# Attention as one tied stream of matmuls in a hybrid layer kernel (scores, transposes and value products in a fixed rotation, output weights per unit)

## The chip, the cores and the metric

One core of a Trainium2 chip runs the whole kernel. The metric is device time in microseconds (us); lower is better. The kernel before was timed three times, and its median is the figure of reference.

## What is computed

One layer over 1024 latent tokens of width 1024 and 256 context tokens: conditioned norm, one input projection, then two groups of heads side by side, one output projection, and a mixture of 16 experts. The part that the change touches is the attention of the latent tokens and what runs beside it:

```python
def attend_blocked(q, k, v):          # 8 query heads, 2 key heads, head width 64, 1280 keys
    ...
    def one_block(qblk):
        s = jnp.einsum('bkgqd,bksd->bkgqs', qblk, k).astype(jnp.float32) * scale
        p = jax.nn.softmax(s, axis=-1).astype(v.dtype)
        return jnp.einsum('bkgqs,bksd->bkgqd', p, v)
...
    # head group B: gated DeltaNet, chunked scan, once per direction
    v_new = u_c - jnp.einsum('bhck,bhkv->bhcv', w_c, s)
    s_next = s * gl_c[..., None, None] + jnp.einsum('bhck,bhcv->bhkv', kd_c, v_new)
    o = jnp.einsum('bhck,bhkv->bhcv', qd_c, s) + jnp.einsum('bhij,bhjv->bhiv', qk_c, v_new)
...
    y = rmsnorm(o, o_norm_w) * jax.nn.silu(z)
    y_lat = jnp.concatenate([att_lat, dn_lat], axis=-1) @ w_out
```

## The kernel before

The kernel is written against a tile framework. Each engine has one queue that it works off strictly in order. The framework fills the queues in the order of the program, except that an instruction whose buffer is not yet free at that point stands back while later instructions of other streams go ahead, so the streams of one engine are mixed. `tc.issue_after` adds an order between two instructions of one engine without a semaphore.

The stages are: modulation and input projection (up to some 405 us), attention beside the DeltaNet scan (to about 705), attention beside the preparation of the output weights (to about 755), attention beside the first four output tiles (to about 870), the other output tiles and the choice of tokens, then the experts.

**Attention** is 16 calls of `att_group(j, hp)`: four blocks of 256 queries times four pairs of heads. A group is four *units* (`i`, `a`), 128 queries of one head each. In a unit TensorE (PE) makes the scores in three pieces (L1153, two matmuls each, into one of four buffers of the PSUM bank "a"), VectorE (DVE) takes each piece to SBUF with its running minimum (L1156, then L1158), ScalarE (ACT) takes the exponential of the whole row (L1159), PE transposes it in pieces of 4, 4 and 2 blocks (L1163, into one of two buffers of bank "t"), and ACT copies each piece out (L1164). At the group's end 20 value products (L1170) add into a buffer of bank "t"; they come in pairs that fill the two halves of the array (`tile_position`). The trace shows each as two instructions. The four `prob` buffers let scores run up to four units in front.

**Queries.** `att_q(j + 1)` is called in the group with `hp == 1` and `j < 3`. `query_split` makes its rotated and split queries by a chain on DVE (L481 to L503, with twelve small instructions of the inverse root between), then PE transposes them in four batches into bank "t" (L1123), the bank that attention's transposes and value products use.

**DeltaNet.** Ten steps `st`, each with two directions (`dn_step`), put on PE per direction the merges (lines 910 to 945, up to 64x64), then L977, L983, L992, L1005 and L1011. Between these stand results of DVE (L979, L988, L996) and ACT. One attention group is written behind each step. `tick` draws pieces of a side stream (`dn_wave`, DVE, lines 868 to 877) in between. From `st == 7` on `dn_out` norms two finished tiles: a sum, squares, an inverse root and a product on DVE (L1032 to L1048), four transposes per tile on PE (L1051), a copy on ACT (L1052) and a store.

**Output weights.** `out_weights` yields 16 pieces. Each loads a 128x512 slice, multiplies it by the gate row on DVE (L1214), takes its upper part on ACT (L1215) and the rest on DVE (L1216). The gate row of each half is loaded and added first (L1210). All 16 pieces are drawn by one `tick(16)` between attention groups 10 and 11 (counted from 0), behind `dn_out(7, 0)`. Groups 12 to 15 run beside `out_next`, which puts the output matmuls of one tile (lines 1298 to 1300) on PE.

Of the kernel before, what the change touches and what calls it, by code (L numbers as in the profile page):

```python
# [10 lines left out]
F32 = mybir.dt.float32  # L11
# [22 lines left out]
P = 128  # L34
# [8 lines left out]
DH = 4  # L43
# [41 lines left out]
class Layer:  # L85
# [51 lines left out]
    def build(self):  # L137
# [20 lines left out]
        for st in range(NT):  # L158
# [862 lines left out]
    def dn_out(self, *tiles):  # L1021
# [61 lines left out]
    def att_open(self):  # L1083
# [5 lines left out]
        self.att = {}  # L1089
# [40 lines left out]
    def att_group(self, j, hp):  # L1130
        nc = self.nc
        v = nc.vector
        tp = self.tp
        if hp == 1 and j < 3:
            self.att_q(j + 1)
        QT, rs = self.att[j]
        if hp == 0:
            self.OT = self.tw.tile([P, 4, 256], F32, name="OT", bufs=1)
        OT = self.OT
        kv = hp // 2  # L1140
        PT = [(self.tw if n == 2 else tp).tile([P, 512 * n], F32, name=f"PT{n}", tag=f"PT{n}", bufs=2)
              .rearrange("p (x a i q) -> p x a i q", x=n, a=2, i=2) for _, n in self.KG]
        for i in range(2):
            for a in range(2):
                h = 2 * hp + a
                pr = self.tw.tile([P, TOK], F32, name="prob", bufs=4)
                mn = self.tw.tile([P, 4], F32, name="mn", bufs=6)
                for y, (tag, c0, w) in enumerate((("a", 0, 448), ("a", 448, 416), ("a", 864, 416))):
                    ps = self.bank(tag)
                    for k0 in range(0, w, 512):  # L1150
                        ks = slice(c0 + k0, c0 + min(k0 + 512, w))
                        for x in range(2):
                            nc.tensor.matmul(ps[:, k0:min(k0 + 512, w)], QT[:, h, i], self.KTs[:, kv * 2 + x, ks],  # L1153
                                             start=x == 0, stop=x == 1)

                    v.tensor_scalar(pr[:, c0:c0 + w], ps[:, :w], -1.0, 3e38, op0=ALU.mult, op1=ALU.min,  # L1156
                                    accum_out=mn[:, y:y + 1])
                v.tensor_reduce(mn[:, 3:4], mn[:, 0:3], axis=AX.X, op=ALU.min)  # L1158
                nc.scalar.activation(pr, pr, AF.Exp, bias=mn[:, 3:4], scale=-1.0, accum_out=rs[:, a, hp, i:i + 1])  # L1159
                for g, (k0, n) in enumerate(self.KG):  # L1160
                    pt = self.bank("t")
                    for x in range(n):
                        nc.tensor.transpose(pt[:, x * P:(x + 1) * P], pr[:, (k0 + x) * P:(k0 + x + 1) * P], self.ident)  # L1163
                    nc.scalar.activation(PT[g][:, :, a, i], pt[:, :n * P].rearrange("p (x q) -> p x q", x=n), AF.Copy)  # L1164
# [643 lines left out]
```

## Time and profile before

| | us |
|---|---|
| three runs | 1531.51, 1533.72, 1539.18 |
| median | 1533.72 |
| the profiled execution | 1532.3 |
| its span, first to last instruction | 1530.6 |

The profiled execution is 1.4 us below the median, and 1.7 us of its time lie around the span. In a profile's row "busy" is time in which the engine works on an instruction, from decode to the last write, so neighbours overlap; the distance between the starts of two rows is what an instruction costs its queue. PE is the matmul engine, PEld its weight load, PEclk the granted share of TensorE's clock of 2.4 GHz.

### The profile page before, as it was taken

What the parts mean: (1) busy time and instruction counts of PE and PEld (TensorE: products, weight loads), DVE (VectorE), ACT (ScalarE), POOL (GpSimd) and SP (SyncE); (2) the same over time, 40 slices, a digit from 0 to 9 for tenths busy, and PEclk for the clock granted to TensorE, in tenths of its full rate; (3) what the DMA queues carried; (4) which work ended last, traced back from release to release, by engine and by line L of the source; (5) the groups of instructions that cost most, each with busy time, mean ns of one, the idle gap of its engine ahead of it and who ended that gap; (6) DMA issues with size and microseconds to landing.
All of it is one profiled execution on the core that took longest, in us unless ns stands there. A gap on an engine that the chain in (4) does not pass through costs nothing.

```text
span 1530.6 us, 25513 instructions
## 1 busy us (share of the span) xinstructions
PE 1446.1 (94%) x9444; PEld 1180.8 (77%) x9444; DVE 1170.2 (76%) x2424; ACT 962.9 (63%) x1602; POOL 167.4 (11%) x184
## 2 busy tenths in 40 slices
PE   4999999998799999999699997999999999999996
PEld 1887687898787878887577774788888888888885
DVE  1834668798685888568743588999999999999995
ACT  1824545654474446667754533788888888888883
POOL 0000000101311121110000101111111111111101
PEclk7899999999999899999899998999999999999998
DMA  9356836788735466554421565989999999999991
GB/s 343 120 182 215 264 119 190 213 280 272 218 102 175 136 182 186 157 172 152 138 70 56 182 245 222 378 296 393 393 398 392 395 395 395 393 387 376 385 377 29
DMA packets 170792, 381.59 MB, mean 249 GB/s; under 512 B 46063, under 2 KB 106235, under 8 KB 143147
## 3 DMA queue, kind: packets, MB, share of 16 engines
q1 hardware_dynamic: 158496, 338.88, 61.9%
q0 software_dynamic: 9792, 37.36, 7.9%
q10 hardware_dynamic: 2379, 3.72, 0.7%
q8 instruction: 74, 1.21, 0.3%
q14 instruction: 51, 0.42, 0.1%
HBM read 324.07 MB, written 55.84 MB: 248 GB/s over the span
## 4 chain that ended last, share of the span: by engine, by line
PE 75%; DVE 9%; DMA 6%; issue 4%; ACT 4%; SPq 1%; POOL 0%; POOLq 0%; ACTq 0%; DVEq 0%
PE ps_m L1631 33%; PE ps_a L1153 4%; PE ps_t L1163 4%; PE ps_t L1170 4%; PE ps_s L444 3%; PE ps_s L446 3%; PE ps_s L445 3%; PE ps_t L1631 2%; PE ps_d L1300 2%; PE ps_d L1298 2%; PE ps_d L1299 2%; PE ps_s L436 1%; PE ps_s L437 1%; PE ps_s L438 1%; PE ps_d L977 1%
## 5 line engine op out<-in xcount | busy, mean ns | idle before, releaser
L1631 PE MATMUL ps_m<-ehi,xx 128*128 128x512 f32 x1024 | 258.0, 394 | 1.0 <-DVE xx L1568 1.0
L1631 DVE TENSOR_TENSOR elo<-eraw,ehi 128x2048 fp32r<-128x2048 f32 x102 | 231.2, 2288 | 18.5 <-ACT ehi L1631 18.0
L1631 ACT ACTIVATE ehi<-eraw 128x2048 fp32r<-128x2048 f32 x105 | 201.3, 1919 | 56.1 <-PE ps_m L1631 43.5
L1631 PEld LDWEIGHTS ps_m<-ehi,xx 128*128 128x128 f32 x1024 | 188.7, 188 | 38.4 <-ACT xf L1564 1.1
L1631 PE MATMUL ps_m<-elo,xx 128*128 128x512 f32 x512 | 137.4, 390 | 0.0
L1631 PE MATMUL ps_m<-ehi,hx 128*128 128x512 f32 x512 | 129.7, 395 | 0.0
L1156 DVE TENSOR_SCALAR_CACHE_REDUCE prob<-ps_a 128x416 f32<-128x416 f32 (+1 forms) x192 | 110.1, 596 | 18.9 <-PE ps_a L1153 14.4
L1631 DVE TENSOR_TENSOR elo<-fraw,ehi 128x2048 fp32r<-128x2048 f32 x51 | 115.8, 2288 | 9.1 <-ACT ehi L1631 9.1
L1164 ACT ACTIVATE PT<-ps_t 128x512 f32<-128x512 f32 (+1 forms) x192 | 93.9, 526 | 38.9 <-PE ps_t L1163 36.8
L1153 PE MATMUL ps_a<-kts,QT 128*128 128x416 f32 (+1 forms) x384 | 111.3, 398 | 5.2 <-DVE prob L1156 5.1
L1631 ACT ACTIVATE ehi<-fraw 128x2048 fp32r<-128x2048 f32 x51 | 97.8, 1918 | 24.1 <-PE ps_m L1631 21.0
L1631 PEld LDWEIGHTS ps_m<-elo,xx 128*128 128x128 f32 x512 | 96.1, 188 | 20.4
L1631 PEld LDWEIGHTS ps_m<-ehi,hx 128*128 128x128 f32 x512 | 94.0, 188 | 18.2
L436 PE MATMUL ps_s<-whi,hh 128*128 128x256 f32 (+1 forms) x336 | 100.0, 299 | 4.1 <-DVE zz L629 4.1
L1163 PE MATMUL ps_t<-consts,prob 128*128 128x128 f32 x640 | 101.1, 285 | 1.0 <-ACT PT L1164 0.6
L438 PE MATMUL ps_s<-whi,hl 128*128 128x256 f32 (+1 forms) x336 | 97.6, 295 | 0.2 <-DVE hl L413 0.2
L437 PE MATMUL ps_s<-wlo,hh 128*128 128x256 f32 (+1 forms) x336 | 97.3, 292 | 0.0
L444 PE MATMUL ps_s<-hh,whi 128*128 128x512 f32 (+1 forms) x256 | 94.6, 370 | 0.0
L1159 ACT ACTIVATE prob<-prob,mn 128x1280 f32<-128x1280 f32 x64 | 87.3, 1365 | 10.4 <-DVE mn L1158 10.1
L446 PE MATMUL ps_s<-hh,wlo 128*128 128x512 f32 (+1 forms) x256 | 93.5, 365 | 0.0
L445 PE MATMUL ps_s<-hl,whi 128*128 128x512 f32 (+1 forms) x256 | 93.5, 365 | 0.0
L1776 POOL DMA_INDIRECT out_x<-ey,idx x16 | 52.0, 3252 | 342.4 <-DVE ey L1631 342.4
(432 smaller groups left out, 3099.0 us busy)
## 6 DMA issues: line engine op xcount, KB each, us to landing
eraw<-in_w_up SPq DMA_DIRECT2D x38, 1024.0 KB, 10.1
eraw<-in_w_down SPq DMA_DIRECT2D x32, 1024.0 KB, 7.4
eraw<-in_w_gate SPq DMA_DIRECT2D x31, 1024.0 KB, 8.7
wmod<-in_w_mod SPq DMA_DIRECT2D x24, 1024.0 KB, 6.1
fraw<-in_w_down SPq DMA_DIRECT2D x21, 1024.0 KB, 8.0
fqraw<-in_w_gate SPq DMA_DIRECT2D x16, 1024.0 KB, 8.9
fraw<-in_w_gate SPq DMA_DIRECT2D x16, 1024.0 KB, 7.0
fraw<-in_w_up SPq DMA_DIRECT2D x14, 1024.0 KB, 10.6
```

The costliest lines, as they stand in the source:

```text
L436: self.nc.tensor.matmul(ps[:, :n], self.hh[:, k, ts], hi[:, k, a:a + n], start=st, stop=False)
L437: self.nc.tensor.matmul(ps[:, :n], self.hh[:, k, ts], lo[:, k, a:a + n], start=False, stop=False)
L438: self.nc.tensor.matmul(ps[:, :n], self.hl[:, k, ts], hi[:, k, a:a + n], start=False, stop=en)
L444: self.nc.tensor.matmul(ps[:, :n], hi[:, k, a:a + P], self.hh[:, k, ts], start=st, stop=False)
L445: self.nc.tensor.matmul(ps[:, :n], hi[:, k, a:a + P], self.hl[:, k, ts], start=False, stop=False)
L446: self.nc.tensor.matmul(ps[:, :n], lo[:, k, a:a + P], self.hh[:, k, ts], start=False, stop=en)
L1153: nc.tensor.matmul(ps[:, k0:min(k0 + 512, w)], QT[:, h, i], self.KTs[:, kv * 2 + x, ks], start=x == 0, stop=x == 1)
L1156: v.tensor_scalar(pr[:, c0:c0 + w], ps[:, :w], -1.0, 3e38, op0=ALU.mult, op1=ALU.min, accum_out=mn[:, y:y + 1])
L1159: nc.scalar.activation(pr, pr, AF.Exp, bias=mn[:, 3:4], scale=-1.0, accum_out=rs[:, a, hp, i:i + 1])
L1163: nc.tensor.transpose(pt[:, x * P:(x + 1) * P], pr[:, (k0 + x) * P:(k0 + x + 1) * P], self.ident)
L1164: nc.scalar.activation(PT[g][:, :, a, i], pt[:, :n * P].rearrange("p (x q) -> p x q", x=n), AF.Copy)
L1631: i = fn(*args, **kw)
```

## The change

The attention is cut into `att_unit`, `att_scores`, `att_rows` (transposes and copies), `att_values` and `att_end`. All its matmuls on PE go through `queue("pa", ...)`, which ties each behind the one before it in the order of the program. The order is a rotation: piece `y` of the scores of a unit, then piece `y` of the transposes of the unit two in front of it. The value products of a group come in the third unit of the next group, behind its first piece of scores. Where values were written as a loop of their own at the group's end, they now run beside the next step of DeltaNet. `dn_out` is cut into `dn_norm` (all that DVE does, the eight products L1050 too) and `dn_rows` (transposes, copy, store). For tiles (7, 0), `dn_rows` is placed behind the last value product that group 11 issues. The output weights are drawn per unit: 1.5 pieces ahead of each unit of group 10 (6 pieces), 2.5 ahead of each of group 11 (10 pieces).

```diff
         self.prep, self.credit = self.out_weights(), 0
-        self.att_group(*ga.pop(0))
-        self.dn_out(7, 0)
-        self.tick(16)
+        self.att_group(*ga.pop(0), 1.5)
+        last = self.dn_norm(7, 0)
         self.close("tq")
-        self.att_group(*ga.pop(0))
+        done = self.att_group(*ga.pop(0), 2.5)
+        with self.tc.issue_after(done.ins):
+            self.dn_rows(*last)
         self.tick(1000)
...
             self.att_group(*ga.pop(0))
+            if not ga:
+                self.att_end()
...
+    def att_group(self, j, hp, aside=0):
...
         if hp == 1 and j < 3:
             self.att_q(j + 1)
...
+        for u in range(4):
+            if aside:
+                self.tick(aside)
+            unit = self.att_unit(j, hp, u // 2, u % 2, PT)
+            old = self.units.pop(0) if len(self.units) == 2 else None
+            for y in range(3):
+                self.att_scores(unit, y)
+                if u == 2 and y == 0 and self.behind:
+                    self.att_values(*self.behind)
+                if old:
+                    self.att_rows(old, y)
+            self.units.append(unit)
+        self.behind = j, hp, PT
+        return self.valued
...
+            self.queue("pa", nc.tensor.matmul, ps[:, :w], QT[:, 2 * hp + a, i], self.KTs[:, hp // 2 * 2 + x, c0:c0 + w],
+                       start=x == 0, stop=x == 1)
...
+            self.queue("pa", nc.tensor.transpose, pt[:, x * P:(x + 1) * P], pr[:, (k0 + x) * P:(k0 + x + 1) * P], self.ident)
...
+                    self.valued = self.queue("pa", nc.tensor.matmul, po[64 * a:64 * a + 64, :256],
+                                             self.V[:, kt, kv * 64:kv * 64 + 64],
```

No engine gets another number of instructions; only the order changes, on PE and DVE above all, between the start of attention and the last value product. In the order of the change all of attention's matmuls bear the line of the helper (L1672), and are told apart by what they read and write: scores `ps_a<-kts,QT`, transposes `ps_t<-consts,prob`, value products `ps_t<-PT,v`. Other lines are 3 higher than before up to `dn_out`.

**Place 1: PE where the queries of the third block are made** (beside DeltaNet's steps 5 and 6). Before:

```order
L938 MATMUL ps_d<-F_4279,mN_6157 64x64 x4
L977 MATMUL ps_d<-S_5865,kqT_6206 128x128 x3
L943 MATMUL ps_d<-q_6191,F_4279 64x64 x4
L977 MATMUL ps_d<-S_5865,kqT_6206 128x128
L1153 MATMUL ps_a<-kts,QT 128x416
L1153 MATMUL ps_a<-kts,QT 128x448 x2
L1153 MATMUL ps_a<-kts,QT 128x416 x4
L983 MATMUL ps_d<-svv_6199,F_4279 128x128 x4
L992 MATMUL ps_d<-vn_6222,skk_6198 128x128 x4
L1005 MATMUL ps_d<-S_5865,kqT_6206 128x128 x4
L1011 MATMUL ps_d<-vn_6222,sqk_6202 128x128 x4
```

With the change:

```order
L1672 MATMUL ps_t<-consts,prob 128x128 x2
L1672 MATMUL ps_a<-kts,QT 128x448 x2
L941 MATMUL ps_d<-F_4279,mN_6102 64x64 x4
L980 MATMUL ps_d<-S_5784,kqT_6151 128x128 x4
L946 MATMUL ps_d<-q_6136,F_4279 64x64 x4
L986 MATMUL ps_d<-svv_6144,F_4279 128x128 x4
L995 MATMUL ps_d<-vn_6167,skk_6143 128x128 x4
L1008 MATMUL ps_d<-S_5784,kqT_6151 128x128 x4
L1014 MATMUL ps_d<-vn_6167,sqk_6147 128x128 x4
```

Scores stood between the DeltaNet products; now none do, in this step and in the next, until all 16 transposes of the queries (L1132, the old L1123) have gone. The next tied matmul is a transpose into bank "t", whose two buffers the queries' transposes hold, and the scores are tied behind it.

DVE at the same place, before:

```order
L1156 TENSOR_SCALAR prob,mn<-ps_a 128x416
L1012 TENSOR_TENSOR otmp<-otmp,ps_d 128x512
L500 TENSOR_TENSOR sr_sp<-sr_sp,sr_b 128x16x64
L1158 TENSOR_REDUCE mn<-mn 128x1
L1156 TENSOR_SCALAR prob,mn<-ps_a 128x448
L1156 TENSOR_SCALAR prob,mn<-ps_a 128x416
L979 SCALAR_TENSOR_TENSOR svv_6304<-ps_d,g_ckb,svv_6304 128x128 x4
L503 TENSOR_TENSOR sr_sp<-sr_sp 128x16x64
L1156 TENSOR_SCALAR prob,mn<-ps_a 128x416
```

With the change (L503 is the old L500, L506 the old L503, L982 the old L979):

```order
L487 TENSOR_TENSOR sr_raw<-sr_raw,rs_r 128x1024
L1015 TENSOR_TENSOR otmp<-otmp,ps_d 128x512
L494 TENSOR_TENSOR sr_sp<-sr_raw,qcs 128x16x64
L501 TENSOR_TENSOR sr_b<-sr_raw,qcs 128x16x16 x3
L982 SCALAR_TENSOR_TENSOR svv_6249<-ps_d,g_ckb,svv_6249 128x128 x4
L501 TENSOR_TENSOR sr_b<-sr_raw,qcs 128x16x16
L1042 COPY orq<-rq 128x4 x2
L991 TENSOR_TENSOR vn_6272<-ps_d,g_bp 128x512
L503 TENSOR_TENSOR sr_sp<-sr_sp,sr_b 128x16x64
L999 SCALAR_TENSOR_TENSOR S_6279<-S_5889,g_egl,ps_d 128x128 x4
L1011 TENSOR_TENSOR otmp<-ps_d,g_egc 128x512
L506 TENSOR_TENSOR sr_sp<-sr_sp 128x16x64
```

The score reduces that stood between have moved behind the chain.

**Place 2: PE at the value products of the last group of the first block.** Before:

```order
L1170 MATMUL ps_t<-PT_5609,v 64x256
L1011 MATMUL ps_d<-vn_5573,sqk_5553 128x128 x4
L1170 MATMUL ps_t<-PT_5609,v 64x256 x7
L1170 MATMUL ps_t<-PT_5610,v 64x256 x8
L1170 MATMUL ps_t<-PT_5611,v 64x256 x4
L1177 MATMUL ps_t<-consts,rs 16x128
```

With the change:

```order
L1672 MATMUL ps_t<-PT_5556,v 64x256
L941 MATMUL ps_d<-F_4280,mN_5817 64x64 x4
L980 MATMUL ps_d<-S_5526,kqT_5866 128x128 x3
L948 MATMUL ps_d<-F_4280,q_5851 64x64 x4
L980 MATMUL ps_d<-S_5526,kqT_5866 128x128
L1672 MATMUL ps_t<-PT_5556,v 64x256 x4
L986 MATMUL ps_d<-svv_5859,F_4280 128x128 x4
L1672 MATMUL ps_t<-PT_5556,v 64x256 x3
L1672 MATMUL ps_t<-PT_5557,v 64x256 x3
L995 MATMUL ps_d<-vn_5882,skk_5858 128x128 x4
L1008 MATMUL ps_d<-S_5526,kqT_5866 128x128 x4
L1672 MATMUL ps_t<-PT_5557,v 64x256
```

One run of value products has become several pieces between DeltaNet's products. Over all 16 groups the order has 20 such pieces before, 4 of them of an odd number of products, and 45 with the change, 14 of them odd.

**Place 3: DVE at the second half of the output weights.** Before (lines 126 to 133 are the inverse root of `dn_out(7, 0)`):

```order
L1210 TENSOR_TENSOR g_8500<-g_8500,woraw 128x512
L1040 TENSOR_TENSOR so<-so,orq 128x8
L1156 TENSOR_SCALAR prob,mn<-ps_a 128x416
L1041 TENSOR_TENSOR so<-so,orq 128x8
L1214 TENSOR_TENSOR woraw<-woraw,g_8500 128x512
L1042 TENSOR_SCALAR so<-so 128x8
L1214 TENSOR_TENSOR woraw<-woraw,g_8500 128x512
L126 TENSOR_SCALAR rs_i<-so 128x8
L128 TENSOR_SCALAR rs_h<-so 128x8
L1216 TENSOR_TENSOR wo1l<-woraw,wo1h 128x512
L127 TENSOR_SCALAR rs_i<-rs_i 128x8
L1216 TENSOR_TENSOR wo1l<-woraw,wo1h 128x512
```

With the change (here the first half; L1255 is the old L1214, L1257 the old L1216, L1183 and L1185 the old L1156 and L1158):

```order
L1183 TENSOR_SCALAR prob,mn<-ps_a 128x416
L1255 TENSOR_TENSOR woraw<-woraw,g_8186 128x512
L1183 TENSOR_SCALAR prob,mn<-ps_a 128x416
L1255 TENSOR_TENSOR woraw<-woraw,g_8186 128x512
L1185 TENSOR_REDUCE mn<-mn 128x1
L1255 TENSOR_TENSOR woraw<-woraw,g_8186 128x512
L1183 TENSOR_SCALAR prob,mn<-ps_a 128x448
L1183 TENSOR_SCALAR prob,mn<-ps_a 128x416 x2
L1255 TENSOR_TENSOR woraw<-woraw,g_8186 128x512
L1185 TENSOR_REDUCE mn<-mn 128x1
L1257 TENSOR_TENSOR wo0l<-woraw,wo0h 128x512 x2
```

The weight pieces no longer stand in a row between the steps of an inverse root; one or two stand between two units' score reduces.

## Rows read from the trace of the kernel before

**Rows 1.** The page: busy time of each engine over the span, with its share and instructions.
```profile
PE 1446.1 (94%) x9444; PEld 1180.8 (77%) x9444; DVE 1170.2 (76%) x2424; ACT 962.9 (63%) x1602; POOL 167.4 (11%) x184
```

**Rows 2.** Busy time of each engine in three stretches: attention beside DeltaNet, beside the weights, beside the first output tiles. Columns: stretch, its length, busy time (instructions) of PE, PEld, DVE, ACT, POOL, granted clock, DMA share, GB/s.
```profile
408.00:705.00 297.00, 291.26 (x2957) 241.59 (x2957) 221.88 (x717) 178.26 (x416) 52.70 (x52) 0.98 0.54 154
705.00:755.00 50.00, 36.27 (x220) 27.68 (x219) 43.10 (x140) 35.79 (x76) 2.17 (x4) 0.83 0.58 191
755.00:870.00 115.00, 114.73 (x775) 89.06 (x775) 50.15 (x183) 62.96 (x120) 7.96 (x14) 1.00 0.22 78
```

**Rows 3.** PE's waits from 408 to 870 us: line waited at, what it waited for, us in total, times, longest.
```profile
PE ps_d L1051 <- DVE zl L1048: 9.3, 1, 9.3
PE ps_a L1153 <- DVE prob L1156: 5.1, 5, 1.6
PE ps_d L992 <- ACT vn L986: 0.9, 2, 0.7
PE ps_d L938 <- ACT F L932: 0.9, 1, 0.9
```

**Rows 4.** Value products on PE and what follows them: start, us, line, operands, array and output, count. First three of the pieces into which one group's products were cut, then a single product and a run of 19 (38 instructions).
```profile
455.59 1.08 PE L1170 MATMUL ps_t<-PT,v 128*64 128x256 f32 x8
456.62 0.67 PE L938 MATMUL ps_d<-F,mN 64*64 64x64 f32 x8
457.23 0.94 PE L977 MATMUL ps_d<-S,kqT 128*128 128x128 f32 x6
...
459.12 1.08 PE L1170 MATMUL ps_t<-PT,v 128*64 128x256 f32 x8
460.13 1.16 PE L983 MATMUL ps_d<-svv,F 128*128 128x128 f32 x8
461.22 1.51 PE L1170 MATMUL ps_t<-PT,v 128*64 128x256 f32 x10
462.66 0.33 PE L1163 MATMUL ps_t<-consts,prob 128*128 128x128 f32 x1
...
515.41 0.65 PE L1170 MATMUL ps_t<-PT,v 128*64 128x256 f32 x2
515.99 1.16 PE L1011 MATMUL ps_d<-vn,sqk 128*128 128x128 f32 x8
517.08 4.53 PE L1170 MATMUL ps_t<-PT,v 128*64 128x256 f32 x38
521.54 0.28 PE L1177 MATMUL ps_t<-consts,rs 128*16 128x128 f32 x1
```

**Rows 5.** Scores and transposes taking turns on PE, columns as in Rows 4.
```profile
719.08 0.38 PE L1163 MATMUL ps_t<-consts,prob 128*128 128x128 f32 x2
719.22 0.64 PE L1153 MATMUL ps_a<-kts,QT 128*128 128x416 f32 x2
719.70 0.60 PE L1163 MATMUL ps_t<-consts,prob 128*128 128x128 f32 x4
720.05 0.45 PE L1153 MATMUL ps_a<-kts,QT 128*128 128x448 f32 x1
```

**Rows 6.** DVE while the queries of the third block are made, and the end of the side stream beside the next: start, us, line, operands, count, idle time ahead and its releaser.
```profile
551.99 1.20 DVE L481 TENSOR_REDUCE sr_s<-sr_b 128x16 f32<-128x1024 f32 x1
...
555.10 0.16 DVE L131 TENSOR_TENSOR rs_a<-rs_i 128x16 f32<-128x16 f32 x1
...
560.33 1.21 DVE L484 TENSOR_TENSOR sr_raw<-sr_raw,rs_r 128x1024 f32<-128x1024 f32 x1
561.47 1.11 DVE L979 SCALAR_TENSOR_TENSOR svv<-ps_d,g_ckb,svv 128x128 f32<-128x128 f32 x4
562.50 1.21 DVE L491 TENSOR_TENSOR sr_sp<-sr_raw,qcs 128x1024 f32<-128x1024 f32 x1
563.63 1.08 DVE L498 TENSOR_TENSOR sr_b<-sr_raw,qcs 128x256 f32<-128x256 f32 x3
565.23 1.12 DVE L996 SCALAR_TENSOR_TENSOR S<-S,g_egl,ps_d 128x128 f32<-128x128 f32 x4 [0.51 <-PE ps_d L992]
566.26 0.69 DVE L1008 TENSOR_TENSOR otmp<-ps_d,g_egc 128x512 f32<-128x512 f32 x1
...
582.37 1.05 DVE L877 COPY L<-T 64x1024 f32<-64x1024 f32 x1
```

**Rows 7.** Three neighbouring stretches; the columns are those of Rows 2.
```profile
515.41:525.35 9.94, 9.89 (x126) 6.98 (x126) 8.72 (x23) 1.00 (x4) 1.48 (x2) 1.00 0.58 184
525.35:535.59 10.24, 10.24 (x50) 9.20 (x51) 7.65 (x20) 4.66 (x11) 3.18 (x4) 0.50 0.44 123
535.59:545.00 9.41, 9.41 (x108) 8.33 (x108) 6.25 (x20) 5.07 (x13) 1.04 (x1) 1.00 0.59 159
```

**Rows 8.** DVE and PE around PE's longest wait, at the weight pieces, columns as in Rows 6.
```profile
745.24 2.19 DVE L1048 SCALAR_TENSOR_TENSOR zl<-of,rs_r,zl 128x128 f32<-128x128 f32 x8
...
745.64 2.31 PE L1051 MATMUL ps_d<-consts,zl 128*128 128x128 f32 x8 [9.26 <-DVE zl L1048]
...
749.29 0.71 PE L1153 MATMUL ps_a<-kts,QT 128*128 128x416 f32 x1 [1.33 <-DVE prob L1156]
```

**Rows 9.** DVE at the output weights, 702 to 755 us, by line and shape: count, busy us and mean ns, idle time ahead and its releasers.
```profile
L1214 DVE TENSOR_TENSOR woraw<-woraw,g 128x512 f32<-128x512 f32 x16 | 10.8, 687 | 1.8 <-DMA woraw<-in_w_out 1.8
L1210 DVE TENSOR_TENSOR g<-g,woraw 128x512 f32<-128x512 f32 x2 | 1.4, 694 | 2.1 <-DMA g<-modrow 1.4 <-DMA woraw<-in_w_out 0.7
```

More of the change, by code (lines that the diff above doesn't have):

```diff
@@ L1019, in dn_out_open, with dn_norm @@
         self.nc.vector.tensor_scalar(self.onw, self.onw, 0.5, None, op0=ALU.mult)
-    def dn_out(self, *tiles):
+    def dn_norm(self, *tiles):
         nc, no = self.nc, self.no
@@ L1044, in dn_out, with dn_rows @@
         v.tensor_tensor(r, r, rq.rearrange("p i h -> p (i h)"), op=ALU.mult)
+        for u in range(2 * DH):
+            i, h = u // DH, u % DH
+            v.scalar_tensor_tensor(z[:, i, h], o[:, i, h], r[:, u:u + 1], z[:, i, h], op0=ALU.mult, op1=ALU.mult)
+        return tiles, o, z
+    def dn_rows(self, tiles, o, z):
+        nc = self.nc
         for i, t in enumerate(tiles):
-            for h in range(DH):
-                u = i * DH + h
-                v.scalar_tensor_tensor(z[:, i, h], o[:, i, h], r[:, u:u + 1], z[:, i, h], op0=ALU.mult, op1=ALU.mult)
             pt = self.bank("d")
@@ L1128 @@
     KG = ((0, 4), (4, 4), (8, 2))
-    def att_group(self, j, hp):
+    def att_group(self, j, hp, aside=0):
+        if hp == 1 and j < 3:
+            self.att_q(j + 1)
+        PT = [(self.tw if n == 2 else self.tp).tile([P, 512 * n], F32, name=f"PT{n}", tag=f"PT{n}", bufs=2)
+              .rearrange("p (x a i q) -> p x a i q", x=n, a=2, i=2) for _, n in self.KG]
+        for u in range(4):
[12 more added lines that the diff above has]
+        return self.valued
@@ L1131, in att_group, with att_end, att_unit, att_scores @@
+    def att_end(self):
+        for unit in self.units:
+            for y in range(3):
+                self.att_rows(unit, y)
+        self.att_values(*self.behind)
+    def att_unit(self, j, hp, i, a, PT):
+        pr = self.tw.tile([P, TOK], F32, name="prob", bufs=4)
+        mn = self.tw.tile([P, 4], F32, name="mn", bufs=6)
+        return j, hp, i, a, PT, pr, mn
+    def att_scores(self, unit, y):
         nc = self.nc
         v = nc.vector
-        tp = self.tp
-        if hp == 1 and j < 3:
-            self.att_q(j + 1)
+        j, hp, i, a, PT, pr, mn = unit
@@ L1137, in att_group, with att_rows, att_values @@
+    def att_rows(self, unit, g):
+        nc = self.nc
+        j, hp, i, a, PT, pr, mn = unit
+        k0, n = self.KG[g]
+        pt = self.bank("t")
+        for x in range(n):
+            self.queue("pa", nc.tensor.transpose, pt[:, x * P:(x + 1) * P], pr[:, (k0 + x) * P:(k0 + x + 1) * P], self.ident)
+        nc.scalar.activation(PT[g][:, :, a, i], pt[:, :n * P].rearrange("p (x q) -> p x q", x=n), AF.Copy)
+    def att_values(self, j, hp, PT):
+        nc = self.nc
+        v = nc.vector
         if hp == 0:
@@ L1139, in att_group @@
         OT = self.OT
+        QT, rs = self.att[j]
         kv = hp // 2
[L1141 to L1164, printed above, removed]
         po = self.bank("t")
```

17 lines of the change are left out of this document (12 added, 5 removed).

## The prediction

> **What bounds the kernel now.** I read the whole first, then the stretch that the diff touches, then single waits. Over the span PE is busy 94% and DVE 76% [rows 1], but an average hides the stages, so the table by stretches decides. Beside DeltaNet PE is busy 291.26 of 297 us, DVE 221.88, ACT 178.26 [rows 2]: PE is the bound, and what a change takes from or adds to PE's queue there goes into the time. Beside the weights PE has 36.27 of 50 us and DVE 43.10, at a granted clock of 0.83 [rows 2]: this stretch belongs to DVE. Beside the first output tiles PE is busy 114.73 of 115 us [rows 2]. PE's waits in all three are few: 9.3 us in one piece for `zl` of the last `dn_norm`, 5.1 us for score reduces on DVE, and two items of 0.9 us in DeltaNet [rows 3]. So a better mix of work can win little outside the stretch of the weights; what it costs PE shows at once. What follows attention works off one order that the change leaves alone, so a shift at 870 us is carried to the end one for one.
>
> **Part 1, value products in pieces.** No product is added, but 25 more pieces stand between other matmuls [place 2]. In a run of 38 instructions one takes 4.46 / 38 = 0.117 us (517.08 to 521.54). A piece of 8 between DeltaNet's products takes 1.03 and 1.01 us where the run would take 0.94; the piece of 10 takes 1.44 where it would take 1.17 [rows 4]. That is 0.07 to 0.27 us a piece, mean 0.14, so 25 x 0.14 = 3.5 us. A product without its partner took 0.58 us (515.41 to 515.99) where its share of a run is 0.23 [rows 4]: 0.35 lost. Ten more odd pieces are at least five more broken pairs, 5 to 6 x 0.35 = 2 us. PE is the bound, so nothing hides this: **+5.5 us**. Bounds: 25 x 0.07 = +1.8, and 25 x 0.27 + 2 = +8.8.
>
> **Part 2, scores and transposes in turn.** Two transposes 0.14 us, two scores 0.48, four transposes 0.35 [rows 5]: a unit is 3 x 0.48 + 0.14 + 2 x 0.35 = 2.28 us, and that row already shows them in turn. Transposes stand two units behind, so they wait for exponentials that are long done, and the tie takes away no more than part of the 5.1 us for score reduces. I take **0**, from -2 to +3: in the last stretch ACT has 62.96 of 115 us [rows 2], which covers what it has to do in bursts; without that cover a transpose waits for bank "t", and behind it now the scores too.
>
> **Part 3, the bare stretch.** At place 1 the tie bites. The transposes need bank "t", which comes behind the queries' transposes, those need the DVE chain, and the scores stand behind the transposes. PE has only DeltaNet's products for two directions: five groups of eight at 1.09 us (460.13 to 461.22) and two merges of 0.61 us (456.62 to 457.23) [rows 4], 6.7 each, 13.4 in all. DVE has in that time the chain: L481 1.20, four of 1.13 (L484 560.33 to 561.47, L491, L500, L503), four L498 of 0.36, thirteen small of 0.16, 9.2 together; then L877 1.05, four groups of four L979 or L996 at 1.03, and five of 0.69 like L1008 [rows 6]: 17.8 in all. Where DVE never waits, PE waits 17.8 - 13.4 = 4.4 us. L996 stands behind two groups of PE and an ACT copy, so DVE waits in each direction too, up to some 2 us: at most 8.4. I take 6.5, the middle. Before, the waits for L986 and L932 and a part of those for score reduces lay here, some 2.5 us [rows 3], because scores filled the gaps; they are inside the 6.5 now. Net **+4 us**, from 0 to +6. Nothing takes this back: units lost here are done later by the same bound engine.
>
> Behind such gaps the granted clock may fall. What the trace shows is 10.24 us at half clock (1.2 GHz) from 525.35 on, between stretches at 1.00, with PE busy 10.24 of 10.24 [rows 7], so without a gap, and busy 9.89 of the 9.94 us ahead of it. The Trainium skill (TensorE: Matmul & The Clock Gate, "HAM oscillation — how this bites in real kernels") has it the other way, that the clock drops behind a wait of PE for data and PE then restarts cold. By that rule the bare stretch would be followed by a cold one, by the row alone not. I put nothing in the sum for it and give it a rival.
>
> **Part 4, weights per unit.** Removed is the pile of pieces that PE waits out: 9.26 us to 745.64, then 1.33 at 749.29 [rows 8]. DVE is full at that time, so what disappears as one wait comes back in part as small waits for score reduces, each now behind a weight piece of 0.69 us [place 3, rows 9]. The stretch cannot be shorter than DVE's 43.10 of 50 us: 6.9 to win at most, if no DVE work leaves it. DVE's waits for loads, 1.8 and 2.1 us [rows 9], hang on DMAs that start no earlier, so 6.9 - 3.9 = 3.0 is the other end. I take **-4 us**, nearer the lower, as the loads stay. If score reduces can move behind 755 us, where DVE has 65 us free [rows 2], the whole 9.26 + 1.33 = -10.6 goes; if the exponentials come late through the pieces of ACT, nothing does: 0. The split `dn_rows` only moves four transposes a tile to a place where `zl` is long ready. Its store is wanted by the later output tiles; queues of SP and POOL keep their order but for some rows: 0.
>
> **Sum.** 5.5 + 0 + 4 - 4 = +5.5 us on the profiled execution's 1532.3: **1538 us**. That execution lies 1.4 us below the median of the runs shown, so against the median of 1533.72 it is +0.28%: no change that can be told, since about 0.5% (7.7 us, 1526.0 to 1541.4) is what a measurement of this kernel can tell from none.
>
> **Rivals.**
> *The waits close.* With work for PE always ready in a fixed rotation, the 9.3 us for `zl` and the 5.1 us for score reduces [rows 3] both go, 14.4 us, and the pieces cost their low bound of 1.8 or up to the 5.5, the bare stretch nothing since DeltaNet's chain fills it: 1532.3 - 14.4 + 5.5 = 1523. For it: DVE has room on both sides of the weights. Against: the 43.10 of 50 us, and the order at place 1. Chance 0.22.
> *The bare stretch falls to half clock* (the other side). PE waits the full 8.4 us at place 1 and what follows runs at half clock as in the row of 10.24 us [rows 7], which at full clock is half of that: +5.1. So 5.5 + 6 + 5.1 - 4 = +12.6: 1545. It decides once the waits of that stretch come in gaps of some us. For it: PE has nothing else in its queue there, and the stretch that holds the gap of 9.26 us has a granted clock of 0.83 [rows 2, 8]. Against: beside DeltaNet the clock is 0.98 on average in spite of its waits [rows 2]. Chance 0.22.
> *Nothing on the path.* DVE's chain at place 1 and the weights cancel and the pieces cost 1.8: 1534. Chance 0.11.
> *Much faster.* PE's weight load is busy 358.33 of 462 us and its matmuls 442.26 (the sums of the three stretches) [rows 2]. If the former were the true load, up to 84 us would be idle, and a better order could win a part: half is 42, so 1490. The starts of neighbouring rows speak against it: PE takes 0.117 us per product in runs, with no holes [rows 4]. Beside it stands a sentence of the Trainium skill (Trainium Kernel Development and Optimization, "Performance Expectations"): matmul busy time is a bad metric, that of LDWEIGHTS a good one. Chance 0.02.
>
> **Chances.** The forecast has 0.43. It lies within 0.5% but for its upper end (0.05 of the 0.43 above 1541.4). Faster by over 0.5%: the first rival and the last, 0.24. Slower: 0.22 + 0.05 = 0.27. Same: 0.38 + 0.11 = 0.49. The forecast's own range, from its terms' nearer bounds, is 1532 to 1543. The range for 8 in 10 reaches into the first rival and over most of the second: **1523 to 1548**.
>
> **What would show it.** Part 1: value products as pieces of 0.1 to 0.3 us more than in a run. Part 2: no wait of a transpose for its exponential. Part 3: PE idle 4 to 8 us in one stretch of some 20 us, ended by DVE's L979, L996 or L506 (the old L503), in which no score runs; wrong if score reduces stand there. Part 4: no wait for `zl`, some waits for score reduces instead, and the stretch of the weights 46 us long instead of 50. The prediction falls if PE's busy time between 408 and 705 us grows by less than 2 us or by more than 9, if more time than 6 us goes at the weights, or if a cold stretch follows place 1.

## The result, and the profile with the change

The change is slower: 1552.27 us in the median of five runs (1550.98 to 1561.69) against 1533.72, a ratio of 1.0144 (95% interval 1.0117 to 1.0171). The forecast was 1538 with a range to 1548; the time lies 4 us above the range. What the second rival named, half clock at the bare stretch of place 1, happened and cost more than it was priced at; the tie cost time in other groups too, which no rival had named.

The profiled execution took 1561.69 us (span 1560.0). Of its distance to the profiled one of before, 6.7 us had arisen before attention began: the first transposes of queries start at 413.2 instead of 406.5 us, behind an order that is the same. From there to the end it is 1146.8 against 1124.1 us, +22.7. All comparisons of stretches below start there.

The page, as in [rows 1]:

```profile
PE 1461.9 (94%) x9444; PEld 1186.8 (76%) x9444; DVE 1179.5 (76%) x2424; ACT 960.5 (62%) x1602; POOL 164.8 (11%) x184
```

Numbers of instructions are the same, and shares to a point; PE's busy time is 15.8 us longer, but the row does not tell where. The stretches tell it. Here they are cut at events: from the first transpose of queries to DeltaNet's last product, and from there to the last value product. Columns as in [rows 2]; PE's idle time is the length less PE's busy time. Before:

```profile
406.50:701.60 295.10, 289.08 (x2939) 239.53 (x2940) 218.57 (x702) 176.05 (x411) 52.70 (x52) 0.98 0.54 154
701.60:863.20 161.60, 147.60 (x967) 114.45 (x965) 93.35 (x330) 101.74 (x200) 6.38 (x11) 0.95 0.32 108
```

With the change:

```profile
413.20:732.20 319.00, 301.98 (x2872) 243.48 (x2873) 221.45 (x690) 171.73 (x403) 47.23 (x48) 0.93 0.49 142
732.20:891.70 159.50, 149.90 (x1031) 115.09 (x1029) 98.11 (x341) 104.43 (x205) 6.36 (x11) 0.99 0.33 110
```

The stretch beside DeltaNet is 23.9 us longer, with 11.0 us more idle time of PE (17.0 against 6.0) and a granted clock of 0.93 instead of 0.98. The rest is 2.1 us shorter and idle for 9.6 instead of 14.0 us: the wait for `zl` is gone. So the loss lies where the forecast put its losses (5.5 and 4 us), and is two and a half times as large.

PE's waits from 408 to 900 us, as in [rows 3]:

```profile
PE ps_t L1672 <- ACT PT L1195: 10.6, 12, 2.4
PE ps_d L941 <- ACT F L931: 3.6, 4, 2.2
...
PE ps_d L920 <- ACT q L917: 2.1, 3, 0.7
PE ps_t L1672 <- ACT prob L1186: 1.7, 2, 0.9
```

The 9.3 us for `zl` and the 5.1 for score reduces are not among them. In their place transposes wait 10.6 us for ScalarE's copies out of bank "t", which was 0.6 us before, and the scores stand behind them in the tie. Most of this wait does not lie where the time was lost: from 732 to 892 us, in the part that became shorter, it is

```profile
PE ps_t L1672 <- ACT PT L1195: 8.1, 7, 2.4
```

Place 1 is the stretch of the queries of the third block. PE there, with the idle time ahead and its releaser at a row's end:

```profile
561.07 0.65 PE L1672 MATMUL ps_a<-kts,QT 128*128 128x448 f32 x2
563.93 0.67 PE L941 MATMUL ps_d<-F,mN 64*64 64x64 f32 x8 [2.21 <-ACT F L931]
564.53 2.08 PE L980 MATMUL ps_d<-S,kqT 128*128 128x128 f32 x8
...
568.11 2.08 PE L986 MATMUL ps_d<-svv,F 128*128 128x128 f32 x8 [0.45 <-ACT F L950]
570.93 2.08 PE L995 MATMUL ps_d<-vn,skk 128*128 128x128 f32 x8 [0.74 <-ACT vn L989]
...
576.76 0.21 PE L920 MATMUL ps_d<-F,q 32*32 32x32 f32 x1 [0.70 <-ACT q L917]
...
578.11 1.09 PE L941 MATMUL ps_d<-F,mN 64*64 64x64 f32 x8 [0.90 <-ACT F L935]
...
583.15 2.05 PE L986 MATMUL ps_d<-svv,F 128*128 128x128 f32 x8 [0.60 <-DVE svv L982]
585.98 2.08 PE L995 MATMUL ps_d<-vn,skk 128*128 128x128 f32 x8 [0.78 <-DVE vn L991]
...
592.71 0.21 PE L920 MATMUL ps_d<-F,q 32*32 32x32 f32 x1 [0.71 <-ACT q L917]
...
595.57 0.66 PE L1672 MATMUL ps_t<-consts,prob 128*128 128x128 f32 x4
```

DVE at the same time:

```profile
573.04 1.12 DVE L999 SCALAR_TENSOR_TENSOR S<-S,g_egl,ps_d 128x128 f32<-128x128 f32 x4 [2.44 <-PE ps_d L995]
...
582.65 1.13 DVE L982 SCALAR_TENSOR_TENSOR svv<-ps_d,g_ckb,svv 128x128 f32<-128x128 f32 x4 [3.34 <-PE ps_d L980]
...
590.41 1.22 DVE L506 TENSOR_TENSOR sr_sp<-sr_sp 128x1024 fp32r<-128x1024 f32 x1
```

And the windows of that stretch, and of two inside it:

```profile
561.30:595.60 34.30, 27.19 (x212) 23.71 (x210) 21.23 (x57) 10.29 (x25) 4.15 (x4) 0.65 0.44 127
564.50:574.80 10.30, 9.10 (x44) 8.36 (x43) 6.83 (x27) 1.79 (x4) 1.04 (x1) 0.50 0.37 105
578.20:591.80 13.60, 12.21 (x71) 10.97 (x72) 7.68 (x20) 1.80 (x3) 2.08 (x2) 0.50 0.39 112
```

No score and no transpose of attention runs from 561.7 to 595.57 us. PE is idle for 7.1 us of it (34.3 less 27.19), close to the 6.5 that the forecast took, but mostly for another engine: 5.7 us are waits for ACT and 1.4 for DVE, which is itself busy for only 21.23 of 34.3 us. And 23.9 us run at half clock, where a group of eight products takes 2.0 us (564.53 to 566.54) instead of the 1.09 of [rows 4]. The two windows hold 21.31 us of PE's work; at full clock it would take half of that, so by this estimate the clock alone cost some 10.7 us. DeltaNet is a chain from PE to DVE or ACT and back, so slower products make DVE wait in turn: 2.44 and 3.34 us, where before two such waits took 0.51 us [rows 6] and 1.03 us (L979 at 571.93). The chain of the queries stands in the same queue of DVE: counted from the first transpose of queries, its last link L506 starts 10.7 us later than before (L503 at 572.98).

This is no chance of one execution. e3 and e14 below have the change's order at place 1; there the stretch without scores takes 32.4 and 32.3 us, at a clock of 0.68 in both.

### The profile page after: what moved, and what is told of

Same layout as the page of the kernel before. It is cut to its first block, busy times and chain, and to the rows that moved or that the text cites. A ratio compares the mean times of both kernels' runs of the same rounds, so it can differ in the third digit from the quotient of the medians.

```text
span 1560.0 us, 25491 instructions
## 1 busy us (share of the span) xinstructions
PE 1461.9 (94%) x9444; PEld 1186.8 (76%) x9444; DVE 1179.5 (76%) x2424; ACT 960.5 (62%) x1602; POOL 164.8 (11%) x184
## 4 chain that ended last, share of the span: by engine, by line
PE 75%; DVE 8%; ACT 7%; DMA 7%; issue 2%; SPq 0%; POOLq 0%; POOL 0%; ACTq 0%; DVEq 0%
PE ps_m L1672 32%; PE ps_t L1672 10%; PE ps_a L1672 3%; PE ps_s L447 3%; PE ps_s L449 3%; PE ps_s L448 3%; ACT prob L1186 2%; PE ps_d L1340 2%; PE ps_d L1339 2%; PE ps_d L1341 2%; PE ps_d L980 1%; PE ps_d L986 1%; PE ps_d L995 1%; PE ps_s L439 1%; PE ps_s L440 1%
## 5 line engine op out<-in xcount | busy, mean ns | idle before, releaser
L1672 PE MATMUL ps_m<-ehi,xx 128*128 128x512 f32 x1024 | 258.1, 394 | 1.0 <-DVE xx L1609 1.0
L1672 DVE TENSOR_TENSOR elo<-eraw,ehi 128x2048 fp32r<-128x2048 f32 x102 | 231.2, 2287 | 18.5 <-ACT ehi L1672 18.4
L1672 ACT ACTIVATE ehi<-eraw 128x2048 fp32r<-128x2048 f32 x105 | 201.1, 1917 | 56.2 <-PE ps_m L1672 43.8
L1672 PEld LDWEIGHTS ps_m<-ehi,xx 128*128 128x128 f32 x1024 | 188.7, 188 | 38.4 <-ACT xf L1605 1.1
L1183 DVE TENSOR_SCALAR_CACHE_REDUCE prob<-ps_a 128x416 f32<-128x416 f32 (+1 forms) x192 | 113.0, 598 | 37.7 <-PE ps_a L1672 35.4
L1672 PE MATMUL ps_m<-elo,xx 128*128 128x512 f32 x512 | 137.4, 390 | 0.0
L1672 PE MATMUL ps_m<-ehi,hx 128*128 128x512 f32 x512 | 129.7, 395 | 0.0
L1672 PE MATMUL ps_a<-kts,QT 128*128 128x416 f32 (+1 forms) x384 | 127.9, 411 | 0.0
L1672 PE MATMUL ps_t<-consts,prob 128*128 128x128 f32 x640 | 112.1, 285 | 13.3 <-ACT PT L1195 9.9
L1672 DVE TENSOR_TENSOR elo<-fraw,ehi 128x2048 fp32r<-128x2048 f32 x51 | 115.8, 2287 | 9.2 <-ACT ehi L1672 8.8
L1672 ACT ACTIVATE ehi<-fraw 128x2048 fp32r<-128x2048 f32 x51 | 97.8, 1918 | 24.2 <-PE ps_m L1672 21.4
L1672 PEld LDWEIGHTS ps_m<-elo,xx 128*128 128x128 f32 x512 | 96.1, 188 | 20.4
L1672 PEld LDWEIGHTS ps_m<-ehi,hx 128*128 128x128 f32 x512 | 94.0, 188 | 18.1
L1672 PEld LDWEIGHTS ps_t<-consts,prob 128*128 128x128 f32 x640 | 79.0, 144 | 37.0 <-ACT PT L1195 19.1
## 6 DMA issues: line engine op xcount, KB each, us to landing
eraw<-in_w_up SPq DMA_DIRECT2D x38, 1024.0 KB, 10.2
```

Source lines behind the costliest of these rows:

```text
L1672: i = fn(*args, **kw)
```

## The experiments

Medians are of five rounds (three for e3 and e7; 4 to 12 runs each), beside the kernel before on the same chip, which ran at 1531.6 to 1532.9 us there; so ratios to it are what compares across runs. Differences given in us are those of the medians; the ratios give up to 3 us more or less, and for e3 4.7 us less.

| run | what | us | ratio to before, 95% interval |
|---|---|---|---|
| change | | 1552.27 | 1.0144, 1.0117 to 1.0171 |
| e1 | queries at the end of their group | 1537.74 | 1.0039, 1.0023 to 1.0055 |
| e2 | no tie | 1535.70 | 1.0017, 0.9999 to 1.0035 |
| e3 | weights in one pile | 1557.79 | 1.0149, 1.0123 to 1.0175 |
| e4 | before, with weights per unit | 1532.39 | 1.0001, 0.9977 to 1.0024 |
| e5 | before, queries at the end | 1532.29 | 1.0001, 0.9978 to 1.0024 |
| e6 | e1 and e2 together | 1527.99 | 0.9978, 0.9958 to 0.9997 |
| e7 | products of step 5 twice | 1558.66 | 1.0169, 1.0128 to 1.0211 |
| e8 | before, value products later | 1547.81 | 1.0088, 1.0057 to 1.0119 |
| e9 | e6 with weights in one pile | 1534.47 | 1.0009, 0.9987 to 1.0031 |
| e10 | DeltaNet step inside the group | 1555.94 | 1.0139, 1.0111 to 1.0166 |
| e11 | e10 and e1 | 1544.58 | 1.0071, 1.0046 to 1.0096 |
| e12 | e10, e1 and e2 | 1529.07 | 0.9968, 0.9948 to 0.9988 |
| e13 | e1 for the third block alone | 1539.69 | 1.0054, 1.0030 to 1.0078 |
| e14 | e1 for the fourth block alone | 1551.26 | 1.0126, 1.0091 to 1.0161 |
| e15 | no tie in four groups | 1546.01 | 1.0090, 1.0055 to 1.0124 |

### The tie and the queries: e1, e2, e5, e6

e1, in `att_group`:

```diff
-        if hp == 1 and j < 3:
-            self.att_q(j + 1)
         PT = ...
...
             self.units.append(unit)
+        if hp == 1 and j < 3:
+            self.att_q(j + 1)
         self.behind = j, hp, PT
```

> The change with one edit: the queries of the next block are made at the end of the group with hp == 1, not at its start, so that the transposes and scores of that group no longer stand behind the queries' transposes. Theory A (the bare stretch with its half clock costs most): the stretch without scores goes, and 8 to 12 us come back, 1541 to 1545 us; half clock between 551 and 592 us goes. Theory B (the tie costs in all of attention): at most 3 us come back, 1549 to 1553. Theory C (the cutting of value products costs most): no gain, 1552 to 1555, since the value products are in 51 pieces here and 22 of them odd.

e2, in `att_open` (`queue` then ties nothing until the experts):

```diff
-        self.tail, self.ordered = {}, True
+        self.tail, self.ordered = {}, False
```

> The change without the tie: the same program order, but attention's matmuls are not chained behind each other on TensorE. Theory A: the bare stretch stays in the order (only its first merges and products get scores beside them), so at most 3 us come back, 1549 to 1553. Theory B (tie): 10 us or more come back, 1542 or less. Theory C (value products, here in 46 pieces with 14 odd): no gain, 1550 to 1554.

e1 gives back 14.5 us and e2 16.6 in the medians. For e1 that is theory A, and a little more than it said. For e2 theory A said 3 at most, and failed; what theory B said came, but B had allowed e1 only 3 us. So neither fits both runs. A second chain for the scores alone, apart from that of transposes and values, gives an order identical to that of e2 on every engine: so what harms is that scores stand behind transposes and value products. Here is PE from DeltaNet's last product of step 4 to that of step 5, the step that holds place 1. Before, the change, e2 and e6, each in its own fence:

```profile
550.80:579.30 28.50, 26.23 (x276) 21.56 (x275) 26.61 (x87) 14.28 (x31) 7.87 (x6) 1.00 0.63 177
```

```profile
551.70:591.10 39.40, 32.65 (x258) 28.64 (x256) 27.69 (x80) 12.53 (x27) 6.93 (x8) 0.66 0.49 145
```

```profile
547.30:579.40 32.10, 27.32 (x239) 22.86 (x237) 28.49 (x88) 14.82 (x31) 6.89 (x7) 0.84 0.55 168
```

```profile
549.10:577.90 28.80, 28.80 (x296) 23.23 (x294) 25.53 (x87) 15.39 (x36) 4.91 (x5) 1.00 0.67 184
```

The change needs 10.9 us more than before for 18 instructions fewer. e2 keeps a stretch without scores in its order, idle for 4.8 us and at a clock of 0.84; e6 has none: 28.80 busy of 28.80 us, at full clock, with 20 instructions more than before.

e5 is e1's edit in the kernel before:

```diff
-        if hp == 1 and j < 3:
-            self.att_q(j + 1)
         QT, rs = self.att[j]
...
         v.tensor_copy(OT[:, hp], po[:, :256])
+        if hp == 1 and j < 3:
+            self.att_q(j + 1)
```

> The kernel before with the one edit of e1: the queries of the next block made at the end of the group with hp == 1. Theory A2 (what e1 won back was the tie's damage at the queries, the scores held behind transposes that wait for bank t): without a tie there is nothing to win, 1530 to 1536 us, the same as before. Rival (the place of the queries is worth time by itself, tie or not): 10 us or more faster than before, 1523 or less.

e6 is e1 and e2 in one kernel.

> The change without the tie and with the queries at the end of the group. Theory A2: both edits take away the same loss, so they do not add up; the stretch without scores of 24 us that the untied one still had goes, with 4.6 us of waits and 3.3 us of half clock, of which some 3 us are left over as gain: 1530 to 1534 us. Rival (two separate losses of 14.5 and 16.6 us): 1521 us.

e5 is the same as before, as theory A2 said: in the order of before, later queries are worth nothing. e6 fits neither theory. It gives back 24.3 us, more than either edit alone and less than their sum of 31.1; at 1527.99 it is 2 us below A2's range, and faster than before with an interval that ends at 0.9997. So A2 is right only in part: the two losses overlap but are not the same. With the queries late the tie still costs 9.75 us (e1 against e6), and without the tie early queries still cost 7.7 us in the new order (e2 against e6); in both pairs the intervals are apart.

### Which place, and where the tie harms: e13, e14, e15

e13 and e14 are e1's edit with `j == 1` or `j == 2` alone; e15 leaves the tie off in some groups:

```diff
+        self.ordered = hp != 1
+        if hp == 1:
+            self.tail.pop("pa", None)
         for u in range(4):
```

> The change with only the queries of the third block made at the end of their group (place 1); those of the second and fourth stay at the start. Theory A2, split by where the lost time lies in the two traces (half clock and waits at place 1 some 12 to 13 us more than before, at the queries of the fourth block some 7 more): 9 to 13 us come back, 1539 to 1543. Rival H (the half clock moves elsewhere with the run and place 1 is worth only its waits): at most 6 come back, 1546 or more.

> The change with only the queries of the fourth block made at the end of their group. Theory A2: 3 to 7 us come back, 1545 to 1549, and place 1 stays as in the change. Rival: nothing comes back, 1551 to 1554.

> The change with the tie taken off in the four groups with hp == 1 alone, where queries are made; the other twelve stay tied. Theory A2 (the tie does harm only where the queries' transposes stand in bank t): most of the 16.6 us of e2 comes back, 1535 to 1541. Rival (the tie costs evenly, a twelfth or so a group): 4 us come back, 1547 to 1550.

Place 1 alone gives back 12.6 us of e1's 14.5 (the ratio falls from 1.0144 to 1.0054), inside A2's range. The queries of the fourth block give back 1.0 us, with overlapping intervals: there the loss was read into the trace and is not shown. Step 5 in e13, then in e14:

```profile
543.30:577.80 34.50, 33.94 (x337) 27.85 (x336) 29.23 (x94) 17.38 (x37) 7.94 (x9) 0.95 0.60 174
```

```profile
545.20:582.00 36.80, 30.04 (x258) 26.23 (x256) 27.19 (x80) 12.49 (x27) 6.55 (x7) 0.72 0.52 154
```

e13 does 337 instructions in 34.5 us with 0.6 us idle; e14 does the 258 of the change, with its idle time of 6.8 us and a clock of 0.72 instead of 0.66. e15 falls between both theories, 6.3 us back. At place 1 it does as much as e2: step 5 takes 31.1 us in e15 and 32.1 in e2, and in both no score runs from 561 to 586 us. So the 10.3 us between e15 and e2, whose intervals are apart, are what the tie of the other twelve groups costs, none of which makes queries; A2 had put that at nothing. Where it is paid is not shown.

### The output weights: e3, e4, e9

e3 puts the change back to one pile, e9 does so with e6, and e4 takes the edit on weights and `dn_norm` alone into the kernel before:

```diff
-        self.att_group(*ga.pop(0), 1.5)
-        last = self.dn_norm(7, 0)
+        self.att_group(*ga.pop(0))
+        self.dn_rows(*self.dn_norm(7, 0))
+        self.tick(16)
         self.close("tq")
-        done = self.att_group(*ga.pop(0), 2.5)
-        with self.tc.issue_after(done.ins):
-            self.dn_rows(*last)
+        self.att_group(*ga.pop(0))
```

> The change with the output weights as before: all 16 pieces in one draw between groups 10 and 11, behind the norm and rows of tiles (7, 0). Theory A and C, with part 4 of the prediction at -4 us: slower by 3 to 7 us than the change, 1555 to 1560. If the weights per unit cost time instead (theory D, waits of transposes for ScalarE's copies behind the weights' copies): faster by 3 us or more, 1549 or less.

> The kernel of e6 (no tie, queries at the end of the group) with the output weights as before, all 16 pieces in one draw. If the weights per unit are worth 5 us in a stream of this kind, as e3 showed for the tied one: 1532 to 1535 us. If they are worth nothing, as e4 showed for the kernel before: 1527 to 1530.

> The kernel before with the weights part alone: attention untied and as before, the pieces drawn 1.5 and 2.5 per unit, and the norm of (7, 0) cut from its rows. By part 4 of the prediction: 4 us faster than before, 1527 to 1532, the wait of 9.26 us gone. Theory D: same as before or slower, 1533 to 1538.

With the pile the change is 5.5 us slower in the median but only 0.8 us by the ratio, e6 6.5 us and 4.7; in both pairs the intervals overlap. The stretch itself shows it better. In e3 it takes 164.2 us against 159.5 in the change, with 3.4 us more idle time:

```profile
724.40:888.60 164.20, 151.17 (x1031) 116.02 (x1029) 99.03 (x341) 104.35 (x205) 6.38 (x11) 0.98 0.31 106
```

From DeltaNet's last product to the last value product, e6 and then e9:

```profile
703.40:856.10 152.70, 147.39 (x999) 111.82 (x999) 93.71 (x327) 103.49 (x205) 6.36 (x11) 1.00 0.33 115
```

```profile
707.40:866.00 158.60, 148.38 (x1001) 113.49 (x999) 93.85 (x327) 104.49 (x205) 6.37 (x11) 0.98 0.32 110
```

5.9 us, of which 4.9 are idle time (5.3 against 10.2). In the kernel before the same edit is worth nothing (by the interval, 3.5 us faster at most). PE's waits of e4 from 700 to 790 us:

```profile
PE ps_t L1171 <- ACT prob L1167: 5.7, 3, 3.1
PE ps_a L1161 <- DVE prob L1164: 5.2, 3, 4.0
```

The wait for `zl` is gone there too, but transposes stand directly behind their own unit's exponential and wait for it. So weights per unit seem to pay only where transposes stand two units behind. This is read from the waits; no run changes that distance alone, and the clock from DeltaNet's last product on is also lower in e4 (0.93, before 0.95).

### The cuts in the value products: e8, e10, e11, e12

e8 moves the value products of the kernel before to the start of the next group (36 more pieces); e10 writes the DeltaNet step inside the group of the change (24 fewer):

```diff
+        if self.behind:
+            self.att_values(*self.behind)
         if hp == 1 and j < 3:
             self.att_q(j + 1)
```

```diff
                 if u == 2 and y == 0 and self.behind:
                     self.att_values(*self.behind)
+                if u == 2 and y == 0 and mid:
+                    mid()
```

where `mid` holds the two calls of `dn_step` and their `tick(3)`. e11 is e10 with e1, e12 is e10 with e1 and e2.

> The kernel before with one edit: the value products of a group are issued at the start of the next group, beside the next DeltaNet step, untied. The order then has 56 pieces of value products, 24 of them odd, instead of 20 and 4. Theory V (part 1 of the prediction, a price per cut): 36 pieces x 0.14 + 10 broken pairs x 0.35 = 8.5 us slower than before, 1536 to 1542 us, and TensorE's value products and DeltaNet products take that much longer from start to start. Rival W (the pieces fill waits of DeltaNet, so the cut is paid by waits): the waits shrink as much as the pieces cost, 1529 to 1534.

> The change with one edit: the DeltaNet step is written inside its attention group, right behind the place of the value products, instead of ahead of the group. The value products then come ahead of the step in the program and stand in 21 pieces, 4 of them odd, instead of 45 and 14; tie, queries and weights stay. Theory V (0.36 us a piece, from the 13.0 us of work from start to start that e8's 36 more pieces added): 24 pieces fewer give back 8 to 9 us, 1542 to 1546. Rival (the cuts cost nothing in the tied stream): 1550 to 1554.

> The tied change with both edits, queries at the end of the group (e1) and the DeltaNet step behind the value products (e10): 19 pieces, no stretch without scores at the queries. If the two losses are separate: e1's 1537.7 less 8 to 11 us, 1526 to 1530. If the tie itself costs beside them: 1533 or more.

> The same without the tie: 28 pieces, 12 of them odd. By the price of 0.36 us a piece against e6 (51 pieces, 1528.0): 8 us less, 1519 to 1523. If the cuts were paid by waits there: 1526 to 1530.

e8 costs 13.5 us by its ratio (8.7 to 18.2), more than theory V's 8.5 and far from rival W. From the first query transposes to DeltaNet's last product it takes 10.6 us longer than before, 1.5 of them idle, at the same clock:

```profile
411.80:717.50 305.70, 298.20 (x2915) 238.85 (x2916) 219.35 (x707) 172.33 (x406) 46.84 (x48) 0.98 0.51 148
```

So cuts cost PE's own time, 13.5 / 36 = 0.37 us a piece by the ratio (0.24 to 0.51), where the forecast had 5.5 / 25 = 0.22 with the broken pairs. Theory V failed in all three tests of the other direction: e10 to e12 have 24, 32 and 23 pieces fewer and gained nothing (1555.9, 1544.6 and 1529.1 where 1542 to 1546, 1526 to 1530 and 1519 to 1523 were expected).

The traces tell the price from the gain. Take each piece of value products from its first start to the start of the row behind it, less the idle time listed in between. Over all groups that is 73.1 us before (20 pieces), 82.8 in e8 (56), 79.0 in the change (45) and 73.7 in e10 (21); 81.7 in e1 and 74.7 in e11; 81.0 in e6 and 76.5 in e12. Each pair gives 0.20 to 0.27 us a piece, whether pieces are added or removed. So the price did come back in e10 to e12, and was lost again elsewhere. The same stretch in e10, and its longest waits from 408 to 900 us:

```profile
407.30:731.30 324.00, 299.60 (x2951) 249.30 (x2951) 225.20 (x729) 180.88 (x415) 49.79 (x52) 0.93 0.49 141
```

```profile
PE ps_t L1675 <- ACT PT L1198: 7.4, 11, 2.3
PE ps_d L942 <- ACT F L932: 7.1, 4, 4.5
PE ps_t L1675 <- ACT prob L1189: 6.5, 5, 1.7
PE ps_t L1675 <- DVE OT L1217: 3.7, 1, 3.7
```

PE is idle for 24.4 us, 7.4 more than in the change: DeltaNet's merges wait for ACT, and transposes for exponentials. In e11 this stretch has a clock of 0.94, in e1 0.97. That the pieces had filled such waits is not shown: e10 also moves DeltaNet against the scores, so it is no pure test of the cuts, and what they cost the change net stays open.

### The clock: e7

e7 issues each product of step 5 twice, for instance:

```diff
-                nc.tensor.matmul(pw[:, h], kT[:, h], S[:, h], start=True, stop=True)
+                [nc.tensor.matmul(pw[:, h], kT[:, h], S[:, h], start=True, stop=True) for _ in range(2 if s == 5 else 1)]
```

> The change with all DeltaNet products of step 5, both directions, issued twice (same operands, same result): 40 more products, 5 groups of 8 instructions each way, 10.9 us at full clock, in the stretch without scores. Theory F (TensorE's clock falls there because of the waits, and products in the waits keep it): the granted clock of the stretch rises from 0.65 to 0.9 or more, and the time moves by -5 to +4 us, 1547 to 1556. Rival G (the clock falls by the kind of work, or the stretch is bound by the time of the products themselves): the clock stays near 0.65 and the time grows by 11 to 20 us, 1563 to 1572.

Neither came in full: the time is 6.4 us above the change's in the median and 3.8 by the ratio, where F allowed 4, and the clock fits neither. PE's stretch without scores at place 1 in e7:

```profile
555.50:594.20 38.70, 33.53 (x251) 31.17 (x250) 21.19 (x58) 9.68 (x21) 6.29 (x6) 0.74 0.42 117
```

The clock is 0.74, between 0.65 and 0.9, idle time is 5.2 us instead of 7.1, and the ratio of 1.0169 is not clear of the change's 1.0144. Of the rise in clock only 0.06 goes beyond the 0.68 that e3 and e14 have without doubled products. What makes the clock fall there is not settled.

## Why the prediction was wrong

**Part 3 failed: it left the clock out of the sum.** Its reading of the order was right: transposes behind bank "t", scores behind transposes. Wrong was the step from there to the price, "net +4 us, from 0 to +6"; e13 gives back 12.6. The sum took DeltaNet's products at 1.09 us a group throughout and put nothing in for the clock. At half clock a group took 2.0 us, some 10.7 us more in all, DVE began to wait for PE, and the stretch became 34 us long instead of some 20. That PE was idle for 7.1 us, where 4.4 to 8.4 were given, is in part luck. The sum let PE wait for a full DVE; the trace has PE waiting for ACT in 5.7 of the 7.1 us and DVE idle for 13 of 34.3. PE's 13.4 us also left out the 32x32 merges and the 16 transposes of the queries (2.1 us, 592.89 to 593.91 and 594.23 to 595.30).

The second rival had the clock (half clock behind the full bare stretch, on the other side), with 0.22 and 1545 us. It was too low because it counted 10 us of half clock, as in [rows 7]; place 1 had 23.9, inside the stretch and not behind it. The argument against it, a clock of 0.98 on average beside DeltaNet [rows 2], was no argument: before, scores filled these waits, and the change takes away just that. The rule of the Trainium skill (TensorE: Matmul & The Clock Gate, "HAM oscillation — how this bites in real kernels") speaks of a cold clock behind waits of PE for data, there for a DMA. Here it agrees in time, half clock from 564.5 us on, right behind a wait of 2.21 us for ACT; the row at 525.35 us without a wait [rows 7] still speaks for another cause beside it.

**Part 2 failed: it put the tie at 0, at most +3.** Exponentials were long done, as said: 1.7 us of waits in all. But the tie of the twelve groups that make no queries costs 10.3 us (e15 against e2), and the whole tie still 9.75 with the queries late (e1 against e6). The waits of transposes for copies out of bank "t", which the forecast had allowed only in the last stretch, are 10.6 us in all, 8.1 of them behind DeltaNet; which waits make up the tie's price was not measured.

**Part 1 was right in size.** +5.5 us were forecast, and the pieces take 5.9 us more in the change (79.0 against 73.1). By its whole time e8 costs more, 0.37 us a piece. But "nothing hides this" is not so the other way round: without the pieces other waits open (e10 to e12).

**Part 4 was right in size, by a condition that it did not name.** -4 us were forecast; the stretch is 4.7 us longer with the pile in e3 and 5.9 in e9, and there is no wait for `zl`. The same edit wins nothing in the kernel before (e4), which the forecast did not see.

Added up, 5.9 + 10.3 + 12.6 - 4.7 is 24.1 us, near the 22.7 between the two traces. The losses overlap (e6), so this is no proof, but the two terms that missed, the tie and place 1, carry most of the error. Two of the signs that the prediction gave for its fall came: PE's busy time beside DeltaNet grew by 12.9 us (289.08 to 301.98), not by 2 to 9, and there were cold stretches at place 1.

**The first rival** (waits for `zl` and score reduces close, 1523 us) was half there: both waits are gone from the list, and with the tie off and the queries moved the kernel comes to 1527.99. The tie and the early queries together cost the change its gain; with the tie alone off, the ratio of 1.0017 (0.9999 to 1.0035) shows none.

## What to carry to other kernels

A tie hands the wait of one link to all behind it: before chaining work that takes buffers from a shared bank, look for every other user of that bank, and read in the order what the engine has left while that user waits. The tie cost some 10 us even in groups that make no queries, so time a tied order against the same order untied. Filler between the links of a serial chain can be worth more than the waits it fills: without it 23.9 of 34.3 us ran at half clock here, where the chain's own products took 2.0 us instead of 1.09, so price a stretch that loses its filler at half clock as well. And a price per cut that the rows show in both directions need not show in the whole time, as other waits can take the gain; e6 and e12, faster than before by 0.2 and 0.3%, kept the rotation and gave up the tie and the early queries.

## What was not expected of the hardware

Half clock came both ways in this case: in before for 10.24 us with PE busy for 10.24 [rows 7], and at place 1 for 10.3 and 13.6 us with 1.2 and 1.4 us idle. Doubling the products in between raised the stretch's clock only from 0.65 (0.68 in e3 and e14) to 0.74. Ahead of the fall at 525.35 us PE had for 2.4 us (522.87 to 525.26) run only matmuls of 16 rows and of 32x32; whether that had to do with the fall, no run tests. Which of the engine's doings makes the clock fall is left open.
